# A feed-forward block on one Trainium2 core: a seven-product up step with chained sums, and a normalization that goes through memory

## The chip, the cores and the metric

The kernel runs on one core of one Trainium2 chip. The metric is the time of one execution on the device, in microseconds (us); a kernel's time is the median of its runs.

## The reference, cut to what matters

One layer of a streaming encoder, 2048 tokens of width 1024. Two token mixers are merged, and x is normalized; then comes the part that the change touches:

```
ffn = square(relu(x @ w_mlp_up + b_mlp_up)) @ w_mlp_down + b_mlp_down     # 1024 -> 4096 -> 1024
x   = layernorm(ALPHA * x + ffn, ln2_g, ln2_b)                            # over the 1024 columns
```

All of it is fp32. The kernel gets fp32 accuracy from TensorE by splitting each operand into a high half and the remainder, and adding three products (high x high, high x low, low x high).

## The kernel before, in words

The engines are TensorE (PE; PEld loads its weights), VectorE (DVE), ScalarE (ACT), GpSimd (POOL) and SyncE (SP), whose queue issues all DMAs. PSUM has four banks for products (`pd`) and four (`pa`) for accumulations and other things. The tile scheduler sets the order of each engine's instructions when the kernel is built, from priorities and its own costs; an engine then runs them in that order, so an instruction that waits holds all behind it.

The mixers and the merge take the first 1931 us. The last merge block (`mix`, `scaled`, `norm`) writes x transposed, in chunks of 128 tokens, to DRAM (`d_x`, `sp["x1"]`), and the accumulators' first values (`d_ac`, `sp["ac"]`).

The feed-forward block (`phase3`) makes three passes over the tokens: 768, 768 and 512, which are 6, 6 and 4 chunks. A pass has 16 units. Unit p takes 256 of the 4096 hidden columns:

- `up` multiplies a 2 x 2 block matrix of x (1024 columns in two halves, the pass's tokens in two halves) by a 2 x 2 block matrix of weights (two `raw` tiles of 128 x 1024) with seven products instead of eight, Strassen's way. Its operands are sums of blocks. The input sums XB1 to XB7 are made once per pass by `load_x1`; the weight sums are made in every unit (`weights`): five of the seven are sums, on POOL (L1302), each then split into halves `wh` (ACT, L171) and `wl` (DVE, L174). Each product is 12 matmuls of 384 (third pass: 256) columns. Its results go together in `part` (ACT copies s4, s5, s2; one POOL difference d1; DVE d2, g, f) and in four `out` (DVE sum, ACT relu and square, ACT and DVE split into `hh`, `hl`).
- `down` multiplies the hidden columns of the unit before by two weight tiles (`whi`, `wlo`) and adds to the accumulators `acc` on DVE (L1361): 12 (third pass: 8) accumulations, each after 6 matmuls of 512 columns. The first unit of a pass has no down step, and the last has one with four halves: 12 matmuls for each accumulation.

At the boundary of two passes, `load_x1` makes the next pass's input sums while the last down step runs, two steps per accumulation (`todo`, `some`): XB4, XB1 and XB6 by DVE into `pa`; XB3 and XB7 by POOL into SBUF; XB2 and XB5 need no sum, and their low halves are POOL's. The finished pass is normalized in place: statistics (`bn_stats`) behind each accumulation; then mean and root for all chunks; then, chunk by chunk, subtraction of the mean on ACT (L1402), product with the gain on POOL (L1403), and scale and shift on DVE (L1407), and the store to the output. The accumulators must be stored before they are loaded for the next pass (L1353), so all of this is issued before the second unit's down step. The last pass does the same per chunk (`finish`) at the kernel's end.

## Time and profile before

| | us |
|---|---|
| median of 3 runs (lowest, highest) | 3402.22 (3399.28, 3404.82) |
| the profiled execution, its own time | 3401.22 |
| its span, from the first to the last instruction | 3399.4 |
| TensorE busy / VectorE / ScalarE / GpSimd | 3269.1 / 2312.5 / 1354.1 / 694.6 |

The page gives averages over the whole span. For what one change is worth, stretches are read one by one: a table of busy time by stretch, and the timeline of an engine, which gives start, duration, operation, tiles (output<-inputs), size, count, and in brackets the idle time ahead of the row with the engine that ended it. In the groups of instructions the columns are the count, busy time and mean of one, then the idle time ahead of them and what ended it.

### The profile page before, as it was taken

To read this page: it belongs to the slowest core of one execution; us is meant where nothing else is said; L and a number is where in the kernel's file an instruction comes from. 1 tells how busy PE (TensorE), PEld (TensorE's weight loads), DVE (VectorE), ACT (ScalarE), POOL (GpSimd) and SP (SyncE) were. 2 spreads that over 40 slices of the span, in tenths; PEclk is the share of its full clock that TensorE was granted. 3 is DMA by queue.
4 is the path that set the end of the run, shared out by engine and by line. 5 is a ranking of instruction groups with operands and counts; after the bars stand their busy time and mean duration, and the time that the engine had idled before them with its cause. 6 is when DMAs were issued, how large, how long until landed. Compare 5 with 4: busy or idle time off the path is not lost.

```text
span 3399.4 us, 51874 instructions
## 1 busy us (share of the span) xinstructions
PE 3269.1 (96%) x20152; PEld 2833.8 (83%) x20152; DVE 2312.5 (68%) x4154; ACT 1354.1 (40%) x2514; POOL 694.6 (20%) x510
## 2 busy tenths in 40 slices
PE   9999999999999999997999989999989999979997
PEld 7778877778888888886999878999879989968886
DVE  5665556565666665655566677776797677799888
ACT  5442454323333332323223353443444444445553
POOL 0120001101000000001333452222253222244432
PEclk9999899999999999998999989999999999989999
DMA  5436434556433544326244441222242212233222
GB/s 161 144 130 176 154 116 140 140 164 200 132 117 120 159 137 128 121 68 214 98 141 140 143 161 50 75 75 74 76 149 75 75 51 74 75 124 125 100 94 74
DMA packets 263190, 405.18 MB, mean 119 GB/s; under 512 B 51324, under 2 KB 161950, under 8 KB 262944
## 3 DMA queue, kind: packets, MB, share of 16 engines
q1 hardware_dynamic: 262944, 401.87, 36.1%
q8 instruction: 158, 2.59, 0.3%
q14 instruction: 88, 0.72, 0.1%
HBM read 291.70 MB, written 110.10 MB: 118 GB/s over the span
## 4 chain that ended last, share of the span: by engine, by line
PE 38%; DVE 9%; issue 2%; POOL 1%; ACT 1%; DMA 1%; DVEq 0%; SPq 0%; ACTq 0%; POOLq 0%
PE pd L164 7%; PE pd L165 7%; PE pd L166 7%; PE pa L164 5%; PE pa L166 5%; PE pa L165 5%; DVE wl L174 2%; DVE hl L174 2%; DVE acc L1361 1%; DMA raw<-in_wu 1%; DVE C L1250 1%; POOL sum L1302 1%; DVE wlo L174 1%; DVE acc L1407 1%; ACT wh L171 0%
## 5 line engine op out<-in xcount | busy, mean ns | idle before, releaser
L1302 POOL TENSOR_TENSOR sum<-raw 128x512 f32<-128x512 f32 x248 | 358.3, 1452 | 887.1 <-DVE wl L174 734.3
L164 PE MATMUL pd<-XH,whi 128*128 128x512 f32 x1216 | 507.3, 417 | 0.0
L165 PE MATMUL pd<-XL,whi 128*128 128x512 f32 x1216 | 482.8, 397 | 0.0
L166 PE MATMUL pd<-XH,wlo 128*128 128x512 f32 x1216 | 482.8, 397 | 0.0
L171 ACT CAST whi<-raw 128x1024 fp32r<-128x1024 f32 (+1 forms) x202 | 198.5, 983 | 680.6 <-PE pa L166 417.1
L1361 DVE TENSOR_TENSOR acc<-acc,pa 128x512 f32<-128x512 f32 x480 | 318.5, 680 | 155.2 <-PE pa L166 154.1
L164 PE MATMUL pa<-whi,hh 128*128 128x512 f32 x960 | 377.3, 394 | 13.2 <-DVE acc L1361 11.7
L165 PE MATMUL pa<-wlo,hh 128*128 128x512 f32 x960 | 376.4, 392 | 3.5 <-DVE wlo L174 3.4
L166 PE MATMUL pa<-whi,hl 128*128 128x512 f32 x960 | 375.7, 392 | 0.0
L174 DVE TENSOR_TENSOR wlo<-raw,whi 128x1024 fp32r<-128x1024 f32 (+1 forms) x202 | 234.5, 1161 | 190.8 <-ACT whi L171 188.1
L164 PEld LDWEIGHTS pd<-XH,whi 128*128 128x128 f32 x1216 | 229.0, 188 | 68.9 <-issue 19.9
L166 PEld LDWEIGHTS pd<-XH,wlo 128*128 128x128 f32 x1216 | 228.7, 188 | 56.2 <-issue 1.8
L165 PEld LDWEIGHTS pd<-XL,whi 128*128 128x128 f32 x1216 | 229.9, 189 | 48.3 <-issue 3.6
L174 DVE TENSOR_TENSOR wl<-sum,wh 128x512 fp32r<-128x512 f32 x240 | 194.8, 818 | 82.8 <-ACT wh L171 82.6
L1082 POOL TENSOR_TENSOR m<-gl 128x256 f32<-128x256 f32 x58 | 48.1, 829 | 896.2 <-DVE gl L1080 845.6
L164 PEld LDWEIGHTS pa<-whi,hh 128*128 128x128 f32 x960 | 180.9, 188 | 59.3 <-DVE acc L1361 20.9
L165 PEld LDWEIGHTS pa<-wlo,hh 128*128 128x128 f32 x960 | 181.1, 189 | 40.8 <-DVE wlo L174 4.4
L166 PEld LDWEIGHTS pa<-whi,hl 128*128 128x128 f32 x960 | 181.0, 189 | 38.4
L171 ACT CAST wh<-sum 128x512 fp32r<-128x512 f32 x240 | 148.4, 619 | 154.3 <-PE pd L165 106.2
L164 PE MATMUL pd<-BH,WBh 128*128 128x256 f32 x512 | 146.2, 286 | 14.0 <-ACT WBh L171 14.0
L174 DVE TENSOR_TENSOR hl<-C,hh 128x384 fp32r<-128x384 f32 (+1 forms) x192 | 150.5, 791 | 0.9 <-ACT hh L171 0.6
L1251 ACT ACTIVATE C<-C,pv 128x384 f32<-128x384 f32 (+1 forms) x192 | 110.9, 578 | 92.0 <-DVE C L1250 91.4
(359 smaller groups left out, 7655.7 us busy)
## 6 DMA issues: line engine op xcount, KB each, us to landing
raw<-in_wu SPq DMA_DIRECT2D x96, 512.0 KB
raw<-in_wd SPq DMA_DIRECT2D x96, 512.0 KB
raw<-in_wf SPq DMA_DIRECT2D x48, 512.0 KB
raw<-in_wm SPq DMA_DIRECT2D x32, 512.0 KB
d_gt<-gt SPq DMA_DIRECT2D x64, 256.0 KB
gl<-d_gt SPq DMA_DIRECT2D x58, 256.0 KB
raw<-in_xT SPq DMA_DIRECT2D x24, 512.0 KB
raw<-in_wv SPq DMA_DIRECT2D x32, 264.0 KB
```

The costliest lines, as they stand in the source:

```text
L164: nc.tensor.matmul(ps, lhsT=lhs[0], rhs=rhs[0], start=first, stop=False)
L165: nc.tensor.matmul(ps, lhsT=lhs[0], rhs=rhs[1], start=False, stop=False)
L166: nc.tensor.matmul(ps, lhsT=lhs[1], rhs=rhs[0], start=False, stop=last)
L171: nc.scalar.copy(hi, src)
L174: getattr(nc, lo_eng).tensor_tensor(lo, src, hi.bitcast(F32), op=ALU.subtract)
L1082: nc.gpsimd.tensor_tensor(m, gt[:, 0, :], gt[:, 1, :], op=ALU.add)
L1250: nc.vector.tensor_tensor(t, x, y, op=ALU.add)
L1251: nc.scalar.activation(t, t, AF.Relu, bias=self.pv("bup", 2 * p + a))
L1302: getattr(self.nc, eng).tensor_tensor(src, block(spec[0]), block(spec[1]), op=spec[2])
L1361: nc.vector.tensor_tensor(a, a, ps, op=ALU.add)
L1407: nc.vector.scalar_tensor_tensor(a, a, rs[:, i:i + 1], gb[1][:, q], op0=ALU.mult, op1=ALU.add)
```

## The change

It changes five things.

1. **The seven products** are another set (Winograd's), which needs four sums a side instead of five, with results that are chained: `ORDER` is now 1, 6, 2, 5, 3, 7, 4. Of the weight sums, 5 and 7 stay on POOL; 6 and 3 are made on DVE from 5, in place.
2. **Weight pairs** 1, 5, 6 and 2 are made ahead of each unit's first product, and the pairs have five buffers instead of four.
3. **Results**: one ACT copy (p1) and three DVE sums (u, v, w); no POOL operation.
4. **Input sums**: four, all on DVE into PSUM, 6 from 5 and 4 from 6; all low halves on DVE.
5. **The last normalization** of the first two passes: the accumulators go to a scratch tensor in DRAM (`d_z`) right after their last accumulation and are reloaded for the next pass. In the next pass, from 12 steps on, each chunk is loaded into an `xr` buffer, its statistics are taken, and it is normalized on DVE alone (subtract and gain in one operation, scale and shift in another) and stored. The last pass's `finish` uses the same two DVE operations. Gain and shift (`gb`) are loaded once. The last down step of the first two passes now goes chunk by chunk.

```diff
-    ORDER = (4, 5, 2, 3, 1, 6, 7)
+    ORDER = (1, 6, 2, 5, 3, 7, 4)
...
-        return [self.W.tile([128, 512], F32R, tag="w" + x, name="w" + x, bufs=4) for x in "hl"]
+        return [self.W.tile([128, 512], F32R, tag="w" + x, name="w" + x, bufs=5) for x in "hl"]
...
         def weights(m):
             ws[m] = [t.rearrange("p (k f) -> p k f", k=4) for t in self.wtile()]
-            t = self.sum() if len(self.WSUM[m]) > 1 else None
-            self.combine(t, self.WSUM[m], block, *ws[m], "gpsimd")
+            if m in (1, 2, 4):
+                src = block({1: (0, 0), 2: (0, 1), 4: (1, 1)}[m])
+            elif m == 7:
+                src = self.sum().rearrange("p (k f) -> p k f", k=4)
+                nc.gpsimd.tensor_tensor(src, block((0, 0)), block((1, 0)), op=ALU.subtract)
+            elif m == 5:
+                chain.append(self.sum().rearrange("p (k f) -> p k f", k=4))
+                src = chain[0]
+                nc.gpsimd.tensor_tensor(src, block((1, 0)), block((1, 1)), op=ALU.add)
+            else:
+                src = chain[0]
+                x, y = {6: (src, block((0, 0))), 3: (block((0, 1)), src)}[m]
+                nc.vector.tensor_tensor(src, x, y, op=ALU.subtract)
+            self.split(src, *ws[m])
...
+        for m in (1, 5, 6, 2):
+            weights(m)
         if not self.T:
-            for m in (4, 5, 2, 3):
-                weights(m)
             yield
+        product(1)
+        yield
+        p1 = part("scalar", "p1", ps[1])
+        product(6)
+        yield
+        u = part("vector", "u", ps[6], p1)
+        product(2)
+        yield
...
+        out(0, 0, ps[2], p1)
+        product(5)
+        yield
+        v = part("vector", "v", ps[5], u)
+        product(3)
+        yield
+        out(0, 1, ps[3], v)
+        product(7)
+        yield
+        w = part("vector", "w", ps[7], u)
+        out(1, 1, ps[7], v)
         product(4)
         yield
+        out(1, 0, ps[4], w)
...
         def step(m):
-            if m in (2, 5):
-                self.combine(None, self.XSUM[m], block, hi, lo, lo_eng="gpsimd")
-            elif m in (3, 7):
-                self.combine(self.wp.tile([128, 512], F32, tag="sum", name="sum", bufs=1), self.XSUM[m], block, hi, lo, "gpsimd")
+            if m in one:
+                src = block(one[m])
             else:
-                self.combine(self.pa(), self.XSUM[m], block, hi, lo)
+                src = t[m] = self.pa().rearrange("p (k n) -> p k n", k=4)
+                nc.vector.tensor_tensor(src, *two[m](), op=ALU.subtract)
+            self.split(src, hi, lo)
...
-                nc.scalar.activation(a, a, AF.Identity, bias=nm[:, i:i + 1])
-                nc.gpsimd.tensor_tensor(a, a, gb[0][:, q], op=ALU.mult)
+                nc.vector.scalar_tensor_tensor(a[:, q], a[:, q], nm, gb[0][:, q], op0=ALU.add, op1=ALU.mult)
...
+        def norm_later(c):
+            got = []
+            def load():
+                got.append(xr())
+                nc.sync.dma_start(got[0], sp["z"][c])
+            def stats(q):
+                if not q:
+                    got.append(T.tile([128, 2, 6], F32, tag="bn", name="bn", bufs=6))
+                nc.vector.bn_stats(got[1][:, q, :], got[0][:, q * 512:q * 512 + 512])
+                if q:
+                    got.extend(norms(c, got[0], got[1]))
+            return [load, lambda: None, lambda: stats(0), lambda: stats(1)] + [lambda x=x: got[2 + x]() for x in range(5)]
...
+                for c in range(nt):
+                    nc.sync.dma_start(sp["z"][c0 + c], acc[c])
+                todo += [lambda: None] * 12 + sum([norm_later(c0 + c) for c in range(nt)], [])
```

The scheduler moves instructions with it. The line numbers of the changed kernel are up to 4 higher. Three places follow, before and after.

GpSimd at the start of the first pass, behind the merge's last `m`; z is the layer before's normalization, `sum` a sum of raw inputs or weights. Before:

```order
L174 TENSOR_TENSOR XB2l<-raw,XB2h 128x4x128
L1302 TENSOR_TENSOR sum<-raw 128x512
L174 TENSOR_TENSOR XB5l<-raw,XB5h 128x4x128
L174 TENSOR_TENSOR XB2l<-raw,XB2h 128x4x128
L1302 TENSOR_TENSOR sum<-raw 128x512 x2
L174 TENSOR_TENSOR XB5l<-raw,XB5h 128x4x128
L1302 TENSOR_TENSOR sum<-raw 128x512
L174 TENSOR_TENSOR XB2l<-xr,XB2h 128x4x128
L1302 TENSOR_TENSOR sum<-xr 128x512
L174 TENSOR_TENSOR XB5l<-xr,XB5h 128x4x128
```

And now:

```order
L1246 TENSOR_TENSOR sum<-raw 128x512
L1131 TENSOR_TENSOR z<-z,g_14647 128x1024 x3
L1132 TENSOR_TENSOR z<-z,b_14648 128x1024
L1242 TENSOR_TENSOR sum<-raw 128x512
L1246 TENSOR_TENSOR sum<-raw 128x512
```

The input sums and the low halves are gone from it; what stays is the layer before's normalization and two weight sums a unit.

VectorE in the last down step of the first pass, around two accumulations; `bn` holds statistics, `pa` is PSUM. Before:

```order
L1361 TENSOR_TENSOR acc_18673<-acc_18673,pa 128x512
L174 TENSOR_TENSOR XB3l<-sum,XB3h 128x4x128
L1363 BN_STATS bn<-acc_18673 128x6
L174 TENSOR_TENSOR XB7l<-sum,XB7h 128x4x128
L1361 TENSOR_TENSOR acc_18674<-acc_18674,pa 128x512
L1302 TENSOR_TENSOR pa<-xr 128x512
L1363 BN_STATS bn<-acc_18674 128x6
```

And now:

```order
L1365 TENSOR_TENSOR acc_18673<-acc_18673,pa 128x512
L1425 BN_STATS bn<-xr 128x6
L174 TENSOR_TENSOR XB5l<-pa,XB5h 128x4x128
L1324 TENSOR_TENSOR pa<-raw,pa 128x512
L1365 TENSOR_TENSOR acc_18674<-acc_18674,pa 128x512
L1425 BN_STATS bn<-xr 128x6
L174 TENSOR_TENSOR XB6l<-pa,XB6h 128x4x128
L1324 TENSOR_TENSOR pa<-raw,pa 128x512
```

The statistics are now those of a chunk that has been to memory and back (`xr`), and all low halves and sums of inputs are VectorE's.

VectorE in the third pass, from the first result of a unit on. Before:

```order
L1260 TENSOR_TENSOR d_29197<-pd,s_29168 128x256
L1250 TENSOR_TENSOR C<-pd,s_29145 128x256
L174 TENSOR_TENSOR wlo<-raw,whi 128x1024
L174 TENSOR_TENSOR hl<-C,hh 128x256
L1260 TENSOR_TENSOR g<-pd,d_29197 128x256
```

And now, in the fourth unit:

```order
L1273 TENSOR_TENSOR u<-pd,p_28631 128x256
L174 TENSOR_TENSOR wl<-sum,wh 128x512
L174 TENSOR_TENSOR wl<-raw,wh 128x512
L1263 TENSOR_TENSOR C<-pd,p_28631 128x256
L1425 BN_STATS bn<-xr 128x6
L1397 BN_AGGR mv<-bn 128x2
L1273 TENSOR_TENSOR v<-pd,u 128x256
L174 TENSOR_TENSOR wl<-raw,wh 128x512
L1398 TENSOR_SCALAR nm<-mv 128x1
L174 TENSOR_TENSOR hl<-C,hh 128x256
L183 TENSOR_SCALAR rs_h<-mv 128x1
L1263 TENSOR_TENSOR C<-pd,v 128x256
```

The normalization of the pass before is spread between the rows of the unit, and the weights' low halves stand elsewhere.

## Rows read from the trace of the kernel before

**Rows 1.** The page: span, then busy time, share and instructions of each engine.

```profile
span 3399.4 us, 51874 instructions
PE 3269.1 (96%) x20152; PEld 2833.8 (83%) x20152; DVE 2312.5 (68%) x4154; ACT 1354.1 (40%) x2514; POOL 694.6 (20%) x510
```

**Rows 2.** Busy time by stretch: start, end, length, then engines, clock, DMA.

```profile
core 0: us, PE busy (x) PEld busy (x) DVE busy (x) ACT busy (x) POOL busy (x), PEclk, DMA share, GB/s
1931.00:1996.00 65.00, 46.12 (x205) 40.42 (x204) 53.47 (x92) 33.27 (x68) 42.63 (x25) 0.82 0.45 169
...
2431.00:2553.00 122.00, 104.97 (x470) 89.25 (x469) 109.83 (x148) 57.41 (x102) 60.08 (x36) 0.93 0.38 138
2956.00:3065.00 109.00, 90.18 (x445) 77.94 (x444) 97.01 (x135) 49.59 (x95) 49.71 (x30) 0.89 0.39 132
3110.00:3350.00 240.00, 234.50 (x1455) 209.11 (x1454) 216.30 (x309) 127.98 (x265) 95.53 (x66) 1.00 0.28 97
```

**Rows 3.** TensorE's timeline: a unit of the first pass, one of the third.

```profile
2183.68 0.34 PE L164 MATMUL pd<-XB4h,wh 128*128 128x384 f32 x1
...
2214.61 0.34 PE L164 MATMUL pd<-XB4h,wh 128*128 128x384 f32 x1
...
2229.18 0.39 PE L164 MATMUL pa<-whi,hh 128*128 128x512 f32 x1
...
3239.43 0.28 PE L164 MATMUL pd<-XB4h,wh 128*128 128x256 f32 x1
...
3249.50 0.39 PE L164 MATMUL pa<-whi,hh 128*128 128x512 f32 x1
...
3261.23 0.28 PE L164 MATMUL pd<-XB4h,wh 128*128 128x256 f32 x1
```

**Rows 4.** TensorE's timeline: first product of a pass's last unit, next pass's third.

```profile
2431.30 0.34 PE L164 MATMUL pd<-XB4h,wh 128*128 128x384 f32 x1
...
2553.42 0.34 PE L164 MATMUL pd<-XB4h,wh 128*128 128x384 f32 x1
...
2955.91 0.34 PE L164 MATMUL pd<-XB4h,wh 128*128 128x384 f32 x1
...
3065.12 0.28 PE L164 MATMUL pd<-XB4h,wh 128*128 128x256 f32 x1
```

**Rows 5.** TensorE's waits, 1940 to 2000 us: total, times, longest.

```profile
PE pd L164 <- ACT wh L171: 11.0, 3, 6.7
PE pd L166 <- DVE wl L174: 7.9, 2, 5.1
```

**Rows 6.** Groups by shape, 3110 to 3350 us, VectorE and GpSimd.

```profile
L174 DVE TENSOR_TENSOR hl<-C,hh 128x256 fp32r<-128x256 f32 x44 | 55.9, 1288 | 0.0
...
L1302 POOL TENSOR_TENSOR sum<-raw 128x512 f32<-128x512 f32 x55 | 82.9, 1523 | 144.4 <-DVE wl L174 118.0 <-DMA raw<-in_wu 26.4
```

**Rows 7.** VectorE's timeline: prices with GpSimd idle.

```profile
3257.45 2.47 DVE L1361 TENSOR_TENSOR acc<-acc,pa 128x512 f32<-128x512 f32 x4
...
3371.86 1.28 DVE L1407 SCALAR_TENSOR_TENSOR acc<-acc,rs,xr 128x1024 f32<-128x1024 f32 x1
...
3378.80 0.16 DVE L190 SCALAR_TENSOR_TENSOR rs<-rs_t,rs 128x1 f32<-128x1 f32 x1
```

**Rows 8.** The tail: VectorE's first, blocked and last row, and GpSimd's.

```profile
3363.27 0.69 DVE L1361 TENSOR_TENSOR acc<-acc,pa 128x512 f32<-128x512 f32 x1 [1.49 <-PE pa L166]
...
3367.84 2.27 DVE L190 SCALAR_TENSOR_TENSOR rs<-rs_t,rs 128x1 f32<-128x1 f32 x1
...
3395.03 1.41 DVE L1407 SCALAR_TENSOR_TENSOR acc<-acc,rs,xr 128x512 f32<-128x512 f32 x2
...
3367.70 2.40 POOL L1403 TENSOR_TENSOR acc<-acc,xr 128x1024 f32<-128x1024 f32 x1 [13.89 <-ACT acc L1402]
```

**Rows 9.** Groups by shape, 2010 to 2430 us: VectorE's accumulations.

```profile
L1361 DVE TENSOR_TENSOR acc<-acc,pa 128x512 f32<-128x512 f32 x166 | 110.9, 682 | 68.2 <-PE pa L166 68.2
```

**Rows 10.** SP's timeline: a store, and the next load into the tile.

```profile
2502.32 0.34 SPq L1410 DMA_DIRECT2D out<-acc  x1
2504.98 0.33 SPq L1353 DMA_DIRECT2D acc<-d_ac  x1
```

More of the change, by code (lines that the diff above doesn't have):

```diff
@@ L260, in build @@
         self.sp["ac"] = [dt(f"d_ac{c}", [128, 1024]) for c in range(NC)]
+        self.sp["z"] = [dt(f"d_z{c}", [128, 1024]) for c in range(NC)]
         self.mixers(xclose)
@@ L1267, in up @@
+        product(5)
[8 more added lines that the diff above has]
+        out(1, 1, ps[7], v)
         product(4)
         yield
-        s4 = part("scalar", "s4", ps[4])
-        product(5)
-        yield
-        s5 = part("scalar", "s5", ps[5])
-        d1 = part("gpsimd", "d1", s4, s5, ALU.subtract)
-        product(2)
-        if not self.T:
-            weights(1)
@@ L1277, in up @@
-        yield
-        s2 = part("scalar", "s2", ps[2])
-        self.hn = [[self.T.tile([128, 768], F32R, tag="h" + x, name="h" + x, bufs=4) for x in "hl"] for _ in range(2)]
-        out(1, 0, ps[2], s4)
-        product(3)
-        yield
-        d2 = part("vector", "d2", ps[3], s2, ALU.subtract)
-        out(0, 1, ps[3], s5)
-        product(1)
-        yield
-        g = part("vector", "g", ps[1], d2)
-        f = part("vector", "f", ps[1], d1)
-        product(6)
-        yield
-        out(1, 1, ps[6], g)
@@ L1292, in up @@
-        product(7)
-        yield
-        out(0, 0, ps[7], f)
-    def combine(self, tmp, spec, block, hi, lo, eng="vector", lo_eng="vector"):
-        if len(spec) == 1:
-            src = block(spec[0])
-        else:
-            src = tmp.rearrange("p (k n) -> p k n", k=4)
-            getattr(self.nc, eng).tensor_tensor(src, block(spec[0]), block(spec[1]), op=spec[2])
-        self.split(src, hi, lo, lo_eng=lo_eng)
+        out(1, 0, ps[4], w)
     def load_x1(self, i, c, tile):
         c0, n = self.passes[i]
-        raw = []
+        nc, raw, t = self.nc, [], {}
@@ L1309, in load_x1 @@
         block = lambda b: raw[b[1]][:, 4 * b[0]:4 * b[0] + 4, :]
+        one = {1: (0, 0), 2: (1, 0), 3: (1, 1)}
+        two = {5: lambda: (block((0, 1)), block((0, 0))), 6: lambda: (block((1, 1)), t[5]),
+               7: lambda: (block((1, 1)), block((0, 1))), 4: lambda: (block((1, 0)), t[6])}
         def load():
@@ L1332, in phase3 @@
         acc = [P.tile([128, 1024], F32, name=f"acc{c}") for c in range(6)]
+        gb = [P.tile([128, 1024], F32, name=f"gb{x}") for x in range(2)]
+        for x in range(2):
+            nc.sync.dma_start(gb[x], A["bc"][3 + x:4 + x, :].to_broadcast([128, 1024]))
         NP = 16
@@ L1350, in down @@
             if c0 is not None:
-                some(len(todo))
                 for c in range(nt):
@@ L1363, in down @@
                     nc.vector.bn_stats(stats[c][:, q, :], a)
+                elif c0 is None and len(hs) > 2:
                     some(2)
@@ L1412, in norms, with scaled, shifted, store @@
-            return mean, root, scaled, shifted, store
+                self.rstd(T, rs, [(mv[:, 1:2], 1e-5, 1.0, slice(0, 1))], 1)
+            def scaled(q=slice(0, 1024)):
+                nc.vector.scalar_tensor_tensor(a[:, q], a[:, q], nm, gb[0][:, q], op0=ALU.add, op1=ALU.mult)
+            def shifted(q=slice(0, 1024)):
+                nc.vector.scalar_tensor_tensor(a[:, q], a[:, q], rs, gb[1][:, q], op0=ALU.mult, op1=ALU.add)
+            def store(q=slice(0, 1024)):
+                nc.sync.dma_start(self.out[c * 128:c * 128 + 128, q], a[:, q])
@@ L1442, in finish @@
                 for q in qs:
-                    scaled(0, q)
+                    scaled(q)
                 root()
                 for q in qs:
-                    shifted(0, q)
-                    store(0, q)
-            if last:
-                load_gb()
+                    shifted(q)
+                    store(q)
+            stats = [T.tile([128, 2, 6], F32, tag="bn", name="bn", bufs=6) for c in range(nt)] if last else None
             down(nt, hs + hn, ws, None, stats, finish if last else None)
```

51 lines of the change are left out of this document (12 added, 39 removed).

## The prediction

> **What bounds the kernel now.** I read the page first, then the busy time of chosen stretches, then TensorE's timeline at the places where a feed-forward pass begins or ends, then VectorE and GpSimd side by side. The page [rows 1] says 96% for TensorE, so all its idle time together is 130 us of 3399.4; a change that leaves the matmuls as they are can take from that, and from what matmuls at the lower clock cost beside idle time. The order shows the same instructions on every engine before the first input sums, so only what follows 1931 us is at stake.
>
> There TensorE's own price per unit can be read off. In the first two passes a unit (one round of seven products and one down step) takes 2214.61 - 2183.68 = 30.93 us, its seven products 2229.18 - 2214.61 = 14.57 us, so the down step's 72 matmuls take 16.36 us, 0.227 each [rows 3]. In the third pass the products take 3249.50 - 3239.43 = 10.07 us; 48 matmuls at 0.227 would make 10.9 and the unit 20.98, but it takes 3261.23 - 3239.43 = 21.80 [rows 3]: 0.82 us is lost in each unit. From the last unit of a pass to the third unit of the next, matmuls need 14.57 + 144 x 0.227 (the last down step has four halves, 32.7) + 14.57 + 30.93 = 92.8 us at the first boundary, and 14.57 + 32.7 + 10.07 + 20.98 = 78.3 at the second. They take 122.1 and 109.2 [rows 4]. So 29.3 and 30.9 us are lost there, in waits and in matmuls behind them at the lower level: the granted clock of these stretches is 0.93 and 0.89 [rows 2]. At the start of the first pass TensorE waits 18.9 us for weight halves [rows 5].
>
> Those four places are where VectorE reads 82 to 90% busy and GpSimd 40 to 66% [rows 2]. A VectorE row there is not all work. In the third pass the subtraction `hl`, 256 wide, reads 1288 ns [rows 6], while four accumulations of twice that width take 2.47 us, 0.62 each [rows 7]; so at least 0.67 us of each of the four `hl` rows of a unit is waiting. The tail shows for what: a GpSimd multiply runs 3367.70 to 3370.10, and a one-element VectorE operation that starts at 3367.84 reads 2.27 us [rows 8], where the same operation alone reads 0.16 [rows 7]. VectorE operations on SBUF stand still while GpSimd works on SBUF. The Trainium skill, SBUF — State Buffer, Who interferes with whom, states this as a lock that the later of the two waits out in full; these rows agree.
>
> **The change, part by part.** Prices: a 512-wide VectorE operation 0.62 us, a 1024-wide one 1.28, a small one 0.16 [rows 7], a GpSimd sum 1.5 [rows 6].
>
> *Weights.* A unit had five GpSimd sums and one GpSimd difference; now two sums. VectorE gets two more operations, +1.2 us a unit; ScalarE loses two copies. In the first two passes this costs nothing: VectorE idles 68.2 us over 166 accumulations in front of those accumulations alone, 12 of them a unit, so 4.9 us a unit [rows 9]. If that cover were gone, 1.2 us in some 28 units would be 34 us. Four of seven weight pairs now stand ready before a unit begins, and a fifth buffer holds one more.
>
> *Start of the first pass.* GpSimd is busy 42.6 of 65 us [rows 2]; the change leaves it one sum, four 1024-wide steps of the layer before and another sum. VectorE gets 9 more operations (5.6 us) but loses GpSimd beside it. Bounds: 5.6 us lost, or the 18.9 us of waits gained. The second half of the wait hangs on the last block's normalization, which stays; I take 8 gained.
>
> *First boundary.* Counting the order's rows by these prices, VectorE's work from the last unit to the third of the next pass grows from about 82 to 93 us: 9 input operations (5.6) and 6 weight sums (3.7), with the twelve statistics and most of the normalization replaced by the first two chunks that come back. Before, it read 109.8 us busy [rows 2], so some 28 us was standing still beside 60.1 us of GpSimd, 0.47 us for each. Now GpSimd has 6 sums, 9 us, hence 4 us. 97 us against 92.8 of matmuls: 4 lost. The second product's weights come from a chain (second half of the raw weights, GpSimd sum, VectorE difference, two halves), whose raw half loads only once the last input buffer is free: 3 us more. ScalarE's and VectorE's waits for each other, in order, 6. So 13 of 29.3 stay, 16 are gained. Bounds 0 and 29.3.
>
> *Second boundary.* VectorE's work stays near 70 us, for only two input chunks instead of three are made and the units are shorter; GpSimd falls from 49.7 us to 9. Work plus 4 stands below 78.3, so what is left is the chain's 3, the two first units where VectorE has more work than TensorE (about 3), and waits in order, 8: 14 of 30.9. Gain 17, bounds 0 and 30.9.
>
> *Third pass.* The normalization of the second pass now lies in its first nine units: per chunk two statistics, two 1024-wide and 15 small operations, 1.2 + 2.6 + 2.4 = 6.2 us. In the six fullest units the order gives VectorE 20.7 us of work a unit; two GpSimd sums at 0.7 each make it 22.1, waits 0.9, so 23.0 against 21.80 now: 7 us lost over six. Bounds: 0.82 a unit gained (5), or 3.4 a unit lost (20), if it waits as now: 216.3 busy of 240 us [rows 2], a tenth idle. The last seven units have 16 us of work, and the 0.82 goes: 5 gained, between 0 and 5.7.
>
> *Tail.* VectorE runs from 3363.27 to 3396.44 [rows 8], of which 28 us is what the new order asks for, with four more 1024-wide operations and no GpSimd beside it. Gain 4.5; between 5 lost (the added four, if nothing was blocked) and 6.
>
> *Memory and queues.* Twelve stores and twelve loads of 512 KB are added, through SP. A store and the next load into the same tile stand 2.66 us apart [rows 10], so accumulators return early, in the last down step. The two rows of gains are now loaded once instead of three times.
>
> **Sum:** 8 + 16 + 17 - 7 + 5 + 4.5 = 43.5. The profiled execution took 3401.2 us (span 3399.4 and 1.8 around it), 1.0 under the median: 3357.7, say **3358 us**. What a measurement can tell from no change is 0.2%, 7 us.
>
> **Rivals.**
> *VectorE becomes the bound.* It is already at 90% in the two boundaries' stretches and in the third pass [rows 2], and gets more. The Trainium skill, Perfetto Trace Analysis, Identifying the Most-Contended Engine, takes occupancy as the measure for VectorE and would have work taken off it, not added; by that rule the kernel gets slower, by the rows on blocking it does not. As a mechanism of this kernel: if the long rows are work and not blocking, the start loses 5.6, the first boundary the 11 us added, the third pass 20, the tail 5, and 5 come back: 3401.2 + 36.6 = 3438 us. It decides from the point where VectorE's time per unit of the third pass passes 21.8. Against it stand the 0.16 that reads 2.27 [rows 7, 8].
> *The queues hold the boundary.* SP works in order, and the next pass's weights now stand behind stores that wait for the last accumulations, and behind reloads that wait for stores. If the raw weights come 10 to 12 us later, 5 instead of 16 and 17 are gained: 3401.2 - 20.5 = 3381 us. For it: 2.66 us for one store [rows 10]; against it: the same queue had stores and reloads in these places already.
> *The normalization does not leave the boundary.* The order puts the first two chunks' statistics between the last accumulations. They wait for a store and a load, and the accumulations behind them wait too. Two chunks at 2 x 2.66 us are 10.6; at one boundary wholly and at the other by half, 16 lost of the 43.5: 3401.2 - 27.5 = 3374 us.
> *All blocking goes.* Start 12, boundaries 24 and 26, third pass without loss 5, tail 6: 3401.2 - 73 = 3328 us.
>
> **How the numbers follow.** Forecast 0.58; VectorE the bound 0.08; queues 0.12; normalization stays 0.10; all blocking goes 0.12. The first rival is left out above; the others reach from 3325 to 3392, which also takes in a start without gain and a third pass at its bad end beside half the boundaries' gain. All but the first are faster by over 7 us, unless two bad ends meet: faster 0.87, within 0.2% 0.05, slower 0.08.
>
> **What would show it.** Right: GpSimd's busy time after 1931 us falls to about a third; `hl` 256 wide reads under 0.7 us; the stretch between the pass's last unit and the third unit of the next falls from 122 to about 106 us and from 109 to about 92; units late in the third pass take 21.0 us, the early ones about 23. Wrong: VectorE still over 1 us for `hl`, or boundaries that stay above 115 us, with waits for DMA or for `bn` in front of the accumulations; or early units of the third pass above 25 us.

## The result and the profile after

The changed kernel takes **3348.64 us** (median of 4 runs, 3344.27 to 3353.50) against 3403.1 of the kernel before on the same chip: ratio **0.9842, 95% interval 0.9825 to 0.9859**, 54 us or 1.6% faster. One execution of no_gpsimd, a run below, took 5987.85 us at a granted clock of 0.843 and is left out of its ratio. The forecast was 3358 us, so the sign was right, the time lies in the range, and 10 us more were gained than summed. The profiled execution took 3344.27 us with a span of 3342.2. That is 57.2 under [rows 1], of which 2.7 lie ahead of the change: GpSimd's last product `m` of the layer before starts at 1929.95 us before and at 1927.23 after, and up to there both kernels do the same.

The page of the kernel after, span and busy times, answers to [rows 1]:

```profile
span 3342.2 us, 51754 instructions
PE 3250.5 (97%) x20152; PEld 2824.9 (85%) x20152; DVE 2285.0 (68%) x4431; ACT 1307.1 (39%) x2401; POOL 333.0 (10%) x269
```

GpSimd's busy time has halved over the whole span (694.6 before); behind 1931 us it fell from 500.1 to 140.3. VectorE runs 277 instructions more and is busy 27.5 us less. The busy time by stretch, columns as in [rows 2], for the two boundaries, the first seven units behind the second one, and the next six:

```profile
2425.00:2531.00 106.00, 98.99 (x476) 87.44 (x475) 91.90 (x183) 50.30 (x91) 8.83 (x6) 0.97 0.49 169
2934.00:3016.00 82.00, 80.08 (x446) 70.63 (x445) 74.94 (x135) 40.94 (x81) 8.53 (x6) 1.00 0.50 174
3016.00:3171.00 155.00, 149.40 (x926) 132.89 (x925) 146.73 (x299) 79.06 (x157) 19.60 (x14) 1.00 0.37 126
3171.00:3297.00 126.00, 126.00 (x794) 114.54 (x793) 104.30 (x181) 67.46 (x133) 15.26 (x12) 1.00 0.30 101
```

In the first boundary VectorE did 183 instructions in 91.9 us where before it needed 109.8 for 148; GpSimd beside it fell from 60.1 us to 8.8. The granted clock rose from 0.93 to 0.97 and from 0.89 to 1.00. In the last six units TensorE is busy without a gap.

TensorE's timeline of the kernel after: the third unit of the first pass, both boundaries from a pass's last unit to the next pass's third (as [rows 4]), the eighth unit behind, and the last unit:

```profile
2023.44 0.34 PE L164 MATMUL pd<-XB1h,wh 128*128 128x384 f32 x1
...
2425.58 0.34 PE L164 MATMUL pd<-XB1h,wh 128*128 128x384 f32 x1
...
2530.42 0.34 PE L164 MATMUL pd<-XB1h,wh 128*128 128x384 f32 x1
...
2934.34 0.34 PE L164 MATMUL pd<-XB1h,wh 128*128 128x384 f32 x1
...
3016.32 0.28 PE L164 MATMUL pd<-XB1h,wh 128*128 128x256 f32 x1
...
3171.30 0.28 PE L164 MATMUL pd<-XB1h,wh 128*128 128x256 f32 x1
...
3297.26 0.28 PE L164 MATMUL pd<-XB1h,wh 128*128 128x256 f32 x1
```

From such rows every kernel here can be cut into stages. The start counts from the last product `m`, the tail from the last unit's first matmul to the end of the span.

| stage, us | before | after | gained | predicted |
|---|---|---|---|---|
| start, to the third unit | 98.1 | 96.2 | 1.9 | 8 |
| first pass | 403.2 | 402.1 | 1.1 | 0 |
| first boundary | 122.1 | 104.8 | 17.3 | 16 |
| second pass | 402.5 | 403.9 | -1.4 | 0 |
| second boundary | 109.2 | 82.0 | 27.2 | 17 |
| third pass, next seven units | 152.5 | 155.0 | -2.5 | -7 (six of them) |
| third pass, next six units | 130.7 | 126.0 | 4.8 | 5 (seven units) |
| tail | 51.0 | 44.9 | 6.1 | 4.5 |
| sum | | | 54.5 | 43.5 |

Where TensorE still waits long for one thing (timeline, rows with a wait above 2.5 us behind 1930 us; in brackets the wait and what ended it):

```profile
1977.96 0.69 PE L164 MATMUL pd<-XB7h,wh 128*128 128x384 f32 x1 [6.69 <-ACT wh L171]
...
1992.14 0.69 PE L164 MATMUL pd<-XB6h,wh 128*128 128x384 f32 x1 [4.42 <-ACT wh L171]
...
2483.17 0.69 PE L164 MATMUL pd<-XB6h,wh 128*128 128x384 f32 x1 [6.08 <-ACT wh L171]
```

Two of the three are the second product's weights, `XB6`, the end of the chain. At the first boundary the chain itself waited for a transfer: SyncE asked for the raw weights at 2473.02, and GpSimd's sum began when they had landed.

```profile
2473.02 1.10 SPq L1229 DMA_DIRECT2D raw<-in_wu  x2
...
2478.70 1.26 POOL L1246 TENSOR_TENSOR sum<-raw 128x512 f32<-128x512 f32 x1 [73.81 <-DMA raw<-in_wu]
```

The other wait belongs to the last product of the first unit, `XB7`. Its cause stands on GpSimd (timeline of the kernel after): the sum for these weights comes behind two steps of the layer before.

```profile
1970.28 2.35 POOL L1131 TENSOR_TENSOR z<-z,g 128x1024 f32<-128x1024 f32 x1 [10.72 <-ACT z L1111]
1972.71 2.34 POOL L1132 TENSOR_TENSOR z<-z,b 128x1024 f32<-128x1024 f32 x1
1975.01 2.25 POOL L1242 TENSOR_TENSOR sum<-raw 128x512 f32<-128x512 f32 x1
```

VectorE's groups by shape from 3016 to 3171 us, against [rows 6]: `hl` now means 500 ns and not 1288.

```profile
L174 DVE TENSOR_TENSOR hl<-C,hh 128x256 fp32r<-128x256 f32 x28 | 13.8, 500 | 3.7 <-ACT hh L171 3.6
```

### The profile page after: what moved, and what is told of

Read it like the earlier page. It is cut to its first block, busy times and chain, and to the rows that moved or that the text cites. A ratio compares the mean times of both kernels' runs of the same rounds, so it can differ in the third digit from the quotient of the medians.

```text
span 3342.2 us, 51754 instructions
## 1 busy us (share of the span) xinstructions
PE 3250.5 (97%) x20152; PEld 2824.9 (85%) x20152; DVE 2285.0 (68%) x4431; ACT 1307.1 (39%) x2401; POOL 333.0 (10%) x269
## 4 chain that ended last, share of the span: by engine, by line
PE 80%; DVE 10%; DMA 4%; issue 2%; ACT 2%; POOL 1%; SPq 0%; POOLq 0%; DVEq 0%; ACTq 0%
PE pd L164 17%; PE pd L165 16%; PE pd L166 16%; PE pa L164 5%; PE pa L165 5%; PE pa L166 5%; PE pa L955 2%; DVE wl L174 1%; PE pa L813 1%; DVE acc L1365 1%; DMA raw<-in_wu 1%; PE pa L843 1%; PE pa L863 1%; PE pa L859 1%; PE pa L835 1%
## 5 line engine op out<-in xcount | busy, mean ns | idle before, releaser
L1365 DVE TENSOR_TENSOR acc<-acc,pa 128x512 f32<-128x512 f32 x480 | 325.4, 685 | 148.2 <-PE pa L166 147.8
L174 DVE TENSOR_TENSOR wlo<-raw,whi 128x1024 fp32r<-128x1024 f32 (+1 forms) x202 | 226.5, 1138 | 168.2 <-ACT whi L171 165.7
L171 ACT CAST wh<-sum 128x512 fp32r<-128x512 f32 x192 | 118.1, 618 | 206.7 <-DVE sum L1250 119.9
L1246 POOL TENSOR_TENSOR sum<-raw 128x512 f32<-128x512 f32 x48 | 63.4, 1321 | 1205.0 <-DMA raw<-in_wu 705.5
L174 DVE TENSOR_TENSOR wl<-sum,wh 128x512 fp32r<-128x512 f32 x192 | 145.3, 758 | 34.8 <-ACT wh L171 32.7
L166 PE MATMUL pd<-BH,WBl 128*128 128x256 f32 x512 | 145.8, 285 | 0.5 <-DVE WBl L174 0.5
L165 PE MATMUL pd<-BL,WBh 128*128 128x256 f32 x512 | 145.7, 285 | 0.0
```

Of the source, the lines that this page charges most:

```text
L165: nc.tensor.matmul(ps, lhsT=lhs[0], rhs=rhs[1], start=False, stop=False)
L166: nc.tensor.matmul(ps, lhsT=lhs[1], rhs=rhs[0], start=False, stop=last)
L171: nc.scalar.copy(hi, src)
L174: getattr(nc, lo_eng).tensor_tensor(lo, src, hi.bitcast(F32), op=ALU.subtract)
L1246: nc.gpsimd.tensor_tensor(src, block((1, 0)), block((1, 1)), op=ALU.add)
L1365: nc.vector.tensor_tensor(a, a, ps, op=ALU.add)
```

## The experiments

Theory: VectorE stood still while GpSimd read SBUF; taking GpSimd's work away gave most of the gain, the normalization's move the rest. Rivals: the move of the normalization is the gain; or what matters is how much work stands on which queue. Twelve kernels ran; the ratio is to the kernel before on the same chip, in each case from 4 or 5 runs. The runs were made on three chips, on which the kernel before took 3397.2, 3397.4 and 3400.4 us, so kernels of different chips are compared by ratio. The stages are those of the table above (the first pass takes 402.1 in all of them but norm_only, 403.6).

| run, us | start | 1st bound. | 2nd pass | 2nd bound. | seven | six | tail | median | ratio, interval |
|---|---|---|---|---|---|---|---|---|---|
| norm_only | 98.8 | 113.2 | 404.3 | 91.2 | 163.7 | 130.7 | 44.7 | 3378.4 | 0.9946, 0.9931 to 0.9961 |
| sums_only | 95.8 | 112.8 | 402.1 | 99.1 | 152.0 | 126.0 | 51.4 | 3371.2 | 0.9925, 0.9910 to 0.9940 |
| pool_reads | 95.1 | 108.2 | 408.4 | 88.1 | 170.4 | 126.0 | 44.8 | 3369.8 | 0.9919, 0.9902 to 0.9935 |
| pool_writes | 96.3 | 105.2 | 403.5 | 83.5 | 154.9 | 126.0 | 45.2 | 3347.2 | 0.9849, 0.9834 to 0.9863 |
| swap | 95.0 | 101.0 | 406.5 | 87.1 | 154.8 | 126.0 | 44.9 | 3345.6 | 0.9844, 0.9830 to 0.9858 |
| spread | 94.5 | 104.9 | 404.4 | 82.4 | 155.5 | 126.1 | 48.7 | 3347.2 | 0.9850, 0.9837 to 0.9864 |
| first_unit | 96.9 | 102.2 | 404.0 | 82.4 | 156.8 | 126.1 | 44.8 | 3347.1 | 0.9851, 0.9837 to 0.9864 |
| no_gpsimd | 97.4 | 103.4 | 402.1 | 81.6 | 147.0 | 126.0 | 45.5 | 3336.6 | 0.9819, 0.9806 to 0.9833 |
| vector_reads | 97.2 | 103.7 | 405.6 | 85.4 | 163.6 | 134.0 | 45.1 | 3367.0 | 0.9902, 0.9889 to 0.9916 |
| no_gpsimd_swap | 97.1 | 97.4 | 402.1 | 84.0 | 147.0 | 126.0 | 46.3 | 3333.8 | 0.9807, 0.9794 to 0.9821 |
| early_seventh | 88.2 | 100.4 | 402.1 | 82.0 | 147.0 | 126.0 | 46.7 | 3328.0 | 0.9788, 0.9775 to 0.9802 |
| all_three | 89.0 | 99.7 | 402.1 | 84.7 | 147.0 | 126.0 | 46.4 | 3325.6 | 0.9781, 0.9767 to 0.9794 |

A stage comes from one execution. Kernels that hardly differ from after in the start read 94.5 to 96.9 there, and at the first boundary first_unit, which does the same there as after, reads 102.2 and after 104.8; so three us in one stage settle nothing.

### The two halves of the change apart

norm_only is before with the changes to the third phase; sums_only is before with those to the up product and its inputs. The lines that tell them apart:

```diff
# norm_only, in the third phase
-                gb.append(xr())
-                nc.sync.dma_start(gb[x], A["bc"][3 + x:4 + x, :].to_broadcast([128, 1024]))
+                    nc.sync.dma_start(sp["z"][c0 + c], acc[c])
+                todo += [lambda: None] * 12 + sum([norm_later(c0 + c) for c in range(nt)], [])
# sums_only, in up and load_x1
-    ORDER = (4, 5, 2, 3, 1, 6, 7)
+    ORDER = (1, 6, 2, 5, 3, 7, 4)
-                self.combine(self.pa(), self.XSUM[m], block, hi, lo)
+                src = t[m] = self.pa().rearrange("p (k n) -> p k n", k=4)
+                nc.vector.tensor_tensor(src, *two[m](), op=ALU.subtract)
```

> The kernel before, with the last part of the change alone: the normalization goes through memory into the next pass; the up product, its sums on GpSimd and the weights' order stay as they were. Theory (most of the 54 us came from GpSimd's reads no longer stopping VectorE): the two boundaries lose some 8 us each of normalization work, the tail 6 us, and the third pass, whose VectorE is still stopped by GpSimd, gives 10 us or more back because it now carries the normalization too: 3380 to 3400 us. Rival (the move of the normalization is the gain): 3345 to 3365 us, the second boundary down from 109 to about 82 us here already.

> The kernel before, with the up product of the change alone (four sums a side, chained outputs, input sums on VectorE, weights ahead); the normalization stays in the boundaries as it was. Theory (GpSimd's reads were the cost): the first boundary falls from 122 to about 112 us, the second from 109 to about 97, late units of the third pass from 21.8 to 21.0, early ones to 21.0 too because no normalization stands beside them; in all 3360 to 3370 us. Rival (the move of the normalization is the gain): 3395 to 3400 us, boundaries at 120 and 107.

Measured, 3378.4 and 3371.2 us. Neither half is the gain alone, so the rival that the normalization's move is all falls. The totals lie 1.6 us below and 1.2 above the theory's ranges, far from the rival's. The theory had the second boundary wrong: moving the normalization out gives 18.0 us there, not 8. Nor does either half hold most of the 54 us: by the ratios they are 18 and 26. The boundaries add up: -8.9 and -9.3 make the first (together -17.3), -18.0 and -10.1 the second (-27.2). In the next seven units they do not: norm_only alone loses 11.2 us, sums_only gains 0.6, and together the loss is 2.5. norm_only's busy time from 3039 to 3202 us shows why the normalization costs more there without the other half (columns as in [rows 2]):

```profile
3039.00:3202.00 163.00, 152.07 (x922) 132.14 (x921) 155.20 (x273) 79.27 (x169) 58.61 (x42) 1.00 0.32 117
```

VectorE is busy 155.2 us with 273 instructions, 26 fewer than the kernel after does in 146.7; GpSimd beside it has 58.6 us instead of 19.6.

The two halves act in different ways. An estimate from the traces: take each VectorE row behind 1931 us and subtract the median of the same operation and shape in no_gpsimd, where GpSimd has next to no work. Summed over the rows with two inputs in SBUF, that is 161.0 us of standing still before, 147.5 in norm_only, 51.8 in sums_only and 50.5 in the kernel after. So sums_only frees VectorE, and norm_only moves work out of the boundaries: at the second one its standing still falls by only 2.4 us (15.6 to 13.2), where the stretch is 18.0 us shorter. The other parts of sums_only, such as weights made ahead and a fifth buffer, were not run by themselves.

### GpSimd reading and GpSimd writing

pool_reads is after with `extra` behind the third, fifth and last product of each unit (the first unit has the last two only: 143 operations). pool_writes has a memory set in the same place, pinned by a one-column ScalarE copy.

```diff
+        def extra(m):
+            t = self.W.tile([128, 512], F32, tag="ex", name="ex", bufs=1).rearrange("p (k f) -> p k f", k=4)
+            nc.gpsimd.tensor_tensor(t, ws[m][0].bitcast(F32), ws[m][1].bitcast(F32), op=ALU.add)
# pool_writes instead
+            nc.scalar.copy(t[:, 0:1], ws[m][1].bitcast(F32)[:, 0, 0:1])
+            nc.gpsimd.memset(t, 0.0)
```

> The kernel after, with three GpSimd operations more in each unit of the up product but the first: each adds two SBUF tiles (128x512) into a scratch tile that nobody reads, about as much as the change took from GpSimd. Nobody waits for them, TensorE, VectorE and ScalarE have the same work as after. Theory (GpSimd reading SBUF stops VectorE): the early units of the third pass grow from 22.3 to 23 or more, the late ones from 21.0 to about 21.8, the cast to hl from under 0.8 to over 1.1 us, both boundaries longer by 5 to 15 us; in all 3365 to 3385 us. Rival (what counted was the work on the engines' own queues, not where GpSimd reads): 3345 to 3352 us, units as after.

> The kernel after, with three GpSimd operations more in each unit of the up product but the first, which only write a scratch tile (128x512, set to zero), each ordered behind a one-column ScalarE copy out of a weight tile so that it stands at the same place as the reads of the run beside it. By the Trainium skill, page SBUF - State Buffer, section Who interferes with whom, only GpSimd's reads stop VectorE: 3345 to 3353 us, units of the third pass 22.3 and 21.0 as after. Rival (any GpSimd work stops VectorE): like the run with reads, scaled by the shorter operation: 3353 to 3370 us.

With reads 3369.8 us, with writes 3347.2 on the same chip: no row waits for the added sums, and the reads cost 22.6 us more than the writes. With them GpSimd is busy 329.7 us behind 1931 us: about half of the 360 us that the change took from it is back, and by the ratios (0.9919 and 0.9842) some 26 of the 54 us gained are lost. The stretch behind the second boundary and the six units behind it, with reads, then the first of the two with writes:

```profile
3031.00:3202.00 171.00, 156.71 (x929) 137.84 (x928) 162.47 (x299) 78.81 (x157) 50.87 (x37) 0.96 0.33 114
3202.00:3328.00 126.00, 126.00 (x794) 114.52 (x794) 104.09 (x181) 67.46 (x133) 38.95 (x30) 1.00 0.30 101
```

```profile
3019.00:3174.00 155.00, 150.85 (x926) 134.17 (x925) 146.72 (x299) 82.76 (x180) 32.20 (x37) 0.99 0.36 126
```

The same 299 VectorE instructions take 146.7 us in the kernel after and beside the writes, 162.5 beside the reads. A set is shorter than a sum (527 against 1299 ns in the groups of the two runs); scaled by that, the 15.4 us that the reads cost in the seven units would be 6.3, and the units are as in after (154.9 against 155.0). The whole is too coarse to add to that: 0.9849 against 0.9842, with intervals that overlap. The rival falls. Which VectorE rows stand still, two groups show, an accumulation from PSUM and a sum of two SBUF tiles, with reads (3031 to 3202 us) and then in no_gpsimd (3016 to 3163 us):

```profile
L1373 DVE TENSOR_TENSOR acc<-acc,pa 128x512 f32<-128x512 f32 x57 | 38.1, 678 | 1.2 <-PE pa L166 1.2
L1250 DVE TENSOR_TENSOR sum<-raw,sum 128x512 f32<-128x512 f32 x8 | 10.2, 1280 | 0.0
```

```profile
L1365 DVE TENSOR_TENSOR acc<-acc,pa 128x512 f32<-128x512 f32 x56 | 38.2, 682 | 1.2 <-PE pa L166 0.3
L1250 DVE TENSOR_TENSOR sum<-raw,sum 128x512 f32<-128x512 f32 x7 | 4.8, 684 | 0.0
```

The sum of two SBUF tiles takes 1280 ns beside the reads and 684 without GpSimd (685 beside the writes); the accumulation does not change. The Trainium skill, SBUF — State Buffer, Who interferes with whom, says that a VectorE operation with two SBUF inputs contends with a GpSimd operation that reads SBUF, and not with one that only writes it; these runs agree. That is narrower than the prediction's wording, by which any VectorE operation on SBUF stands still.

Three numbers expected for the reads missed. The first boundary is 3.4 us longer and not 5 or more. The six late units stay at 21.0 each, though GpSimd is busy 39 us in them, and `hl` means 523 ns in the seven units and not over 1100. So it is not GpSimd's time that costs but what falls beside it. How a late unit lost its 0.82 us before, three rows of that kernel show, of VectorE, GpSimd and TensorE:

```profile
3253.98 2.34 DVE L174 TENSOR_TENSOR hl<-C,hh 128x256 fp32r<-128x256 f32 x2
...
3252.93 3.11 POOL L1302 TENSOR_TENSOR sum<-raw 128x512 f32<-128x512 f32 x2 [2.56 <-DVE wl L174]
...
3256.97 0.50 PE L164 MATMUL pa<-whi,hh 128*128 128x512 f32 x1 [0.47 <-DVE acc L1361]
```

Two GpSimd sums lay over two `hl`, the accumulation queued behind those was late, and the down step waited for it. In the late units of pool_reads little of GpSimd's time falls on such rows. Of its 39.2 us there, 4.6 lie beside VectorE rows with two SBUF inputs, 18.4 beside rows that read PSUM, and 16.2 beside idle VectorE; in the seven units it is 31.1 of 51.2 beside two SBUF inputs. The accumulations mean 682 ns in the late units with the reads, and 682 in no_gpsimd. The same section of the Trainium skill says that a VectorE operation with at most one SBUF input, outside its 2-port performance modes (faster modes that also take the ports it shares with GpSimd), does not contend with GpSimd, and the two means agree.

### No GpSimd sums at all, and the same reads on VectorE

```diff
# no_gpsimd
-                nc.gpsimd.tensor_tensor(src, block((0, 0)), block((1, 0)), op=ALU.subtract)
+                nc.vector.tensor_tensor(src, block((0, 0)), block((1, 0)), op=ALU.subtract)
-                nc.gpsimd.tensor_tensor(src, block((1, 0)), block((1, 1)), op=ALU.add)
+                nc.vector.tensor_tensor(src, block((1, 0)), block((1, 1)), op=ALU.add)
# vector_reads, against pool_reads
-            nc.gpsimd.tensor_tensor(t, ws[m][0].bitcast(F32), ws[m][1].bitcast(F32), op=ALU.add)
+            nc.vector.tensor_tensor(t, ws[m][0].bitcast(F32), ws[m][1].bitcast(F32), op=ALU.add)
```

> The kernel after with the last two GpSimd sums of a unit on VectorE too: behind the start of the first pass GpSimd has no work, VectorE 1.3 us more in each unit. Theory (a GpSimd sum of 1.32 us holds VectorE up by about as long as the sum costs VectorE itself, 0.62 us, or more): no change or some us faster; at the start the 6.7 us wait of the last weights, whose GpSimd sum stands behind the layer before's normalization, goes; early units of the third pass the same or up to 0.3 us shorter; ratio 0.981 to 0.984. Rival (VectorE is now the bound, and what it gets costs in full where it is full): early units of the third pass 0.6 to 1.3 us longer each, boundaries 4 us longer each, ratio 0.986 to 0.989.

> The kernel after with the same three added operations in each unit as in the run with GpSimd's reads (a sum of two SBUF tiles, 128x512, into a scratch tile that nobody reads), now on VectorE. Theory (an operation costs VectorE 0.62 us where it runs there, and more than that where it runs on GpSimd and reads SBUF): the seven early units of the third pass together 160 to 166 us, between after's 155.0 and the 170.4 of the run with reads on GpSimd; late units 21.0; boundaries 1 to 4 us longer each; in all 3355 to 3364 us. Rival (VectorE is the bound there, so that work on it costs more than work beside it): 3370 us or more, above the run with GpSimd's reads.

no_gpsimd: 0.9819, where after has 0.9842, some 8 us less, though the two intervals overlap by 0.0008. The stages are clearer: the seven units fall from 155.0 to 147.0 us, 1.1 each, where at most 0.3 was expected. Three windows, the first boundary, the seven units behind the second, and the six behind those:

```profile
2429.00:2532.00 103.00, 96.56 (x468) 85.93 (x467) 92.21 (x188) 48.58 (x90) 0.00 (x0) 0.97 0.50 169
...
3016.00:3163.00 147.00, 147.00 (x926) 133.60 (x925) 143.87 (x310) 79.41 (x155) 0.00 (x0) 1.00 0.39 128
3163.00:3289.00 126.00, 126.00 (x795) 114.51 (x794) 111.05 (x197) 67.22 (x134) 0.00 (x0) 1.00 0.32 106
```

VectorE does 14 sums more in the seven units, is 98% busy, and TensorE does not wait at all: 147.0 busy of 147. This also prices the standing still. By the reckoning above, row against row of the same shape, VectorE's rows of two SBUF inputs stand still 8.9 us in the seven units of after beside 19.6 of GpSimd, 0.45 for each; in pool_reads 24.3 beside 50.87, 0.48. In the six late units it is 2.7 us in both, beside 15 and beside 39. What did not come is the start: there the wait grew (below).

vector_reads: 3367.0 us, 3 above what the theory allowed and 3 under the rival. The seven units lose 8.7 us where GpSimd's reads lost 15.4, as expected. But the six late units lose 8.0, which no theory expected, and the first boundary is 1.1 shorter and not 1 to 4 longer. Four waits of TensorE make 3.8 of the 8.0; the longest:

```profile
3315.44 0.60 PE L164 MATMUL pa<-whi,hh 128*128 128x512 f32 x1 [1.85 <-DVE acc L1373]
```

As before the change, the accumulation ahead of the down step is late. It is not the two GpSimd sums that are still there: beside them VectorE's rows stand still 3.1 us in these six units, and 2.7 in after. That leaves the added operations themselves, by their work or their place in VectorE's order (119.2 us busy of 134); which of the two, and where the other 4.2 us went, is not shown. What stands: in the seven full units the same three operations cost less on VectorE (8.7) than on GpSimd (15.4), in the six others more (8.0 against 0), and the intervals of the two ratios overlap.

### Exchange, spreading, and the first unit

```diff
# swap: the second and third product
+        product(2)
+        yield
         product(6)
         yield
         u = part("vector", "u", ps[6], p1)
-        product(2)
-        yield
# spread
-                todo += [lambda: None] * 12 + sum([norm_later(c0 + c) for c in range(nt)], [])
+                todo += [lambda: None] * 12 + sum([norm_later(c0 + c) + [lambda: None] * 5 for c in range(nt)], [])
# first_unit, for both weight sums
-                nc.gpsimd.tensor_tensor(
+                (nc.gpsimd if self.T else nc.vector).tensor_tensor(
```

> The kernel after with the second and third of the seven products exchanged: the product on a weight block as it was loaded now stands ahead of the product whose weights come from the chain (second raw half, GpSimd sum, VectorE difference, two halves). Theory (TensorE at the first boundary, 104.8 us against 92.8 of matmuls, waits for that chain: 6.1 us in one piece; at the start 4.4 us in one piece): 2 us more of cover there, and the start and the first boundary together come 3 to 5 us earlier, the rest as after: ratio to the kernel before about 0.983. Rival (the chain is late because the last input buffer comes free late, and whatever stands second waits for the same transfer): no change, ratio 0.984 to 0.985.

> The kernel after with the deferred normalization spread out: five empty turns between the chunks, so that a chunk's 6.2 us of VectorE work falls into every second unit of the next pass rather than into each. Theory (the early units of the third pass, 21.4 to 23.1 us against 21.0, are VectorE's: 125.7 of 134 us busy): these units fall to 21.0 to 21.7 us each, 4 to 7 us less in all, both boundaries as after: ratio about 0.982. Rival (the loss comes from the reloads or from the order of the queues, not from VectorE's work): the same 8 us over more units, ratio 0.984 to 0.985.

> The kernel after with the two GpSimd weight sums on VectorE in the first unit of the first pass alone. Theory (the 6.7 us wait for the last product's weights at the start is their GpSimd sum standing behind 7 us of the layer before's normalization on GpSimd): the wait goes, the third unit begins 4 to 6 us earlier, ratio about 0.983. Rival (the wait only moves to the layer before's chain or to the raw weights' transfer): the start as after, ratio 0.984 to 0.985.

None of them moved the ratio from 0.984 by more than its interval. **swap** gained 3.9 us at the first boundary, gave 2.6 back in the units behind it and 5.1 at the second boundary. **spread** did not spread. The scheduler that writes out each engine's order placed the chunks where they were; first and last of the six `xr<-xr,nm,gb` of the second pass's normalization on VectorE, in the kernel after and then in spread:

```profile
2970.84 1.28 DVE L1404 SCALAR_TENSOR_TENSOR xr<-xr,nm,gb 128x1024 f32<-128x1024 f32 x1
...
3127.83 1.28 DVE L1404 SCALAR_TENSOR_TENSOR xr<-xr,nm,gb 128x1024 f32<-128x1024 f32 x1
```

```profile
2968.34 1.28 DVE L1404 SCALAR_TENSOR_TENSOR xr<-xr,nm,gb 128x1024 f32<-128x1024 f32 x1
...
3126.19 1.27 DVE L1404 SCALAR_TENSOR_TENSOR xr<-xr,nm,gb 128x1024 f32<-128x1024 f32 x1
```

So it tells nothing on what spreading is worth. Its tail of 48.7 us against 44.9 stays unexplained. **first_unit** failed as an experiment too: the last product's weights are made when the pass has begun and `self.T` is set, so only the chain's sum moved, and the wait for `XB7` reads 6.75 us as it did.

### The start, and the parts together

In no_gpsimd the wait of the last product of the first unit became longer, and VectorE's rows say what its sum stood behind:

```profile
1984.52 0.69 PE L164 MATMUL pd<-XB7h,wh 128*128 128x384 f32 x1 [10.02 <-ACT wh L171]
...
1974.10 2.64 DVE L1125 TENSOR_SCALAR x<-pa,pv 128x128 f32<-128x128 f32 x8 [2.72 <-PE pa L1121]
1976.66 2.77 DVE L1131 TENSOR_TENSOR z<-z,g 128x1024 f32<-128x1024 f32 x1
1979.46 1.22 DVE L1132 TENSOR_TENSOR z<-z,b 128x1024 f32<-128x1024 f32 x1
...
1981.54 0.68 DVE L1242 TENSOR_TENSOR sum<-raw 128x512 f32<-128x512 f32 x1
```

early_seventh is no_gpsimd with that sum made with the first four weights; no_gpsimd_swap has the exchange of swap; all_three has both.

```diff
-                src = self.sum().rearrange("p (k f) -> p k f", k=4)
+                src = (self.sum() if self.T else self.pa()).rearrange("p (k f) -> p k f", k=4)
-        for m in (1, 5, 6, 2):
+        for m in (1, 5, 6, 2) if self.T else (1, 5, 6, 2, 7):
```

> The kernel without GpSimd sums, with the second and third product exchanged as well. Theory (the exchange covers part of the chain's 6.4 us at the first boundary; in the run of the exchange alone its gain of 3.8 us there was mostly given back in the next unit, where GpSimd's sums stood beside a full VectorE): the gain stays, the first boundary falls from 103.4 to about 101 us, the next units stay at 30.9: 2 us less than without the exchange, ratio about 0.981. Rival (the unit behind is long because VectorE's work is only moved there): no difference, 0.982.

> The kernel without GpSimd sums, with the last product's weights of the first unit made ahead of it (a fifth prepared pair; the difference goes to PSUM). In the run without GpSimd sums TensorE waited 10.0 us in one piece for these weights, whose sum stood behind 8 us of the layer before's work in VectorE's order. Theory (the wait is an order of work and not a shortage): that wait goes, the third unit begins 5 to 8 us earlier, the rest as without GpSimd sums: ratio 0.979 to 0.981. Rival (the next unit's raw weights arrive late anyway): the wait moves to the second unit's first weights, 0 to 2 us gained, ratio 0.981 to 0.982.

> No GpSimd sums, the early seventh weights and the exchanged products together. If the gains are of different places they add up: start 5 to 8 us, first boundary 2 us below the run without GpSimd sums, ratio 0.978 to 0.980. If the start's gain is only moved: 0.981 to 0.982.

early_seventh: 0.9788, the start 9.2 us shorter than without it. The sum and TensorE's third unit in this run:

```profile
1960.04 0.69 DVE L1242 TENSOR_TENSOR pa<-raw 128x512 f32<-128x512 f32 x1
...
2019.42 0.34 PE L164 MATMUL pd<-XB1h,wh 128*128 128x384 f32 x1
```

The sum stands at 1960 and no longer at 1982, though the layer before ended 1.9 us later in this execution. The wait was order, not shortage; the rival falls. no_gpsimd_swap: 0.9807 against 0.9819, intervals that overlap. By stage it gains 6.0 us at the first boundary, where 2.4 were expected, and loses 2.4 at the second. But that boundary reads 100.4 in early_seventh, which does the same there as no_gpsimd (103.4), and 99.7 in all_three, which has the exchange besides; so what the exchange is worth is not shown. all_three: 0.9781, 3325.6 us, the fastest here. By the two ratios it is at 0.9781 / 0.9842 = 0.9938 of the kernel after, about 21 us; against early_seventh the intervals overlap.

## Why the prediction was right, and where not

**What bounds.** Right: that VectorE's operations stand still beside GpSimd was the ground of the whole forecast. pool_reads, pool_writes and no_gpsimd show it from three sides. What they show is narrower: rows of two SBUF inputs, beside GpSimd operations that read SBUF.

**Weights in the first two passes, at no cost.** Right. A unit takes 30.93 us in after, and with two more sums on VectorE in no_gpsimd too.

**Start, 8.** Wrong, 1.9. The first half of the wait did go: in front of the first products TensorE waited 6.9 us before and 1.0 after. But the layer before's last matmuls now wait 3.0 us for VectorE's input sums in PSUM (three waits that end from 1950.85 to 1955.03), a term that the text had only in its lower bound. The second half stayed, as said, at other places: 11.8 us before, 12.1 after. The sum of the last product's weights stayed on GpSimd and behind the layer before, and the second unit's chain got a wait of its own, 4.4 us. Some nine us could be had there, as early_seventh shows, by order alone.

**First boundary, 16.** 17.3, but two of the parts are off and cancel, which is luck. VectorE was busy 91.9 us and not 97, below the 92.8 of matmuls; row against row it stood still 22 us before and 2.6 after, where the text had 28 and 4. The chain cost 6.1 and not 3: 1.6 us until the raw weights had landed, and 4.5 for the sums and halves behind them.

**Second boundary, 17.** 27.2, the largest miss. VectorE's 74.9 us are the 70 and 4 of the text. What failed is what was added to the matmuls: chain 3, first units 3 and waits in order 8, together 14; 82.0 less 78.3 leaves 3.7. Guessing eight us of waits once VectorE's work fits below TensorE's was wrong. norm_only has 18.0 of the gain from the normalization's leaving, sums_only 10.1. With the first boundary 1.3 above and this one 10.2, the boundaries make up for the start's 6.1 too little.

**Early third pass, -7.** -2.5 over seven units. The sums' 0.7 was near (8.9 us of standing still beside 14 sums, 0.64 each). The work was oversized: 146.73 less 8.9 over seven units are 19.7 a unit, against 20.7 counted for the six fullest. The text's lower bound is wrong by its own rows: 22.1 us at 216.3 of 240 busy are 24.5, so 2.7 a unit and 16 over six, not 3.4 and 20; with that the rival of VectorE as the bound gives 3434 us and not 3438.

**Late third pass, 5.** 4.8, and the units stand at 21.0. **Tail, 4.5.** 6.1, and only norm_only of the halves has it (44.7 against 51.4). The text's 28 us for VectorE is what the rows give, from the first accumulation to the last scale and shift:

```profile
3311.30 0.69 DVE L1365 TENSOR_TENSOR acc<-acc,pa 128x512 f32<-128x512 f32 x1 [0.60 <-PE pa L166]
...
3337.78 1.42 DVE L1407 SCALAR_TENSOR_TENSOR acc<-acc,rs,gb 128x512 f32<-128x512 f32 x2
```

**Rivals.** VectorE was not the bound: early units take 22.1 us on average, not above 25, and fall to 21.0 with more work on it. The Trainium skill, Perfetto Trace Analysis, Identifying the Most-Contended Engine, would find the bottleneck by occupancy (time spent in instructions) and optimize that engine first; no_gpsimd put work on VectorE, at 146.73 of 155 us, and these units were faster. The queues held the first boundary by at most the chain's 6.1 us, and in the second no wait is above 2.5; the normalization left both. Of the signs named ahead, GpSimd's busy time fell to 28% (a third was said), `hl` to 500 ns, and the boundaries and units stand in the table.

## What to carry to other kernels

A busy VectorE row is not work until it has been set beside GpSimd's rows of the same microseconds: a 256-wide row of 1288 ns was 0.42 us of work (419 ns in no_gpsimd). Where VectorE looks full beside a GpSimd that reads SBUF, VectorE can be the cheaper place for GpSimd's operation; where it has idle time, as in the six late units here, it was the dearer one. Before a wait at a stage's start is put down to a shortage, look at what stands ahead of the awaited instruction on its own engine; a place earlier in that order gave 9 us here.

## What was not expected of the hardware

GpSimd's reads cost VectorE 0.45 to 0.48 us for each of their own in one stretch and next to nothing more in the next, with the same operations: 50.87 us of GpSimd beside 24.3 us of standing still, then 38.95 beside 2.7, no more than 15.26 cost there in after. And VectorE could be filled to 143.87 us of 147 without one wait on TensorE, once GpSimd no longer read SBUF. Executions differ by some us ahead of the change: the last `m` starts at 1925.86 in spread and at 1931.22 in early_seventh, under the same instructions.
